# Stick-breaking scores: the second pass on half the rows, two key stretches in two halves of the array

## The chip, the cores and the metric

The kernel runs on one core of a Trainium2 chip, as one program. A core has five engines with instruction queues of their own: TensorE (PE in the profile; its weight loads are listed apart as PEld), VectorE (DVE), ScalarE (ACT), GpSimd (POOL) and SyncE (SP, which here only issues DMAs). They run side by side and wait for each other through semaphores. The metric is the device time of one execution in microseconds (us), the median of several runs. Before the change it is 1746.15 us (three runs, 1745.22 to 1746.89).

## The reference

The kernel is one decoder block on 1024 tokens of width 1024 in float32: three attention branches, gated and merged, and a squared-ReLU MLP. The change touches the first branch, stick-breaking attention, with 8 heads of 64 columns:

```python
def stick_breaking_attention(q, k, v):
    for i in range(s_len // BLOCK_Q):          # 8 tiles of 128 queries
        q0 = i * BLOCK_Q
        kend = q0 + BLOCK_Q
        z = einsum('bhtd,bhsd->bhts', q[:, :, q0:kend], k[:, :, :kend]) * HD ** -0.5
        strict = s_idx < t_idx
        log_rem = where(strict, log_sigmoid(-z), 0.0)
        after = cumsum(log_rem, reverse=True) - log_rem
        w = where(strict, exp(log_sigmoid(z) + after), 0.0)
        outs.append(einsum('bhts,bhsd->bhtd', w, v[:, :, :kend]))
```

Query tile i needs the scores of the keys 0 to 128(i+1), so tiles 0 to 3 need at most 512 keys and tiles 4 to 7 need 640 to 1024. The other branches are forgetting attention (8 heads, a softmax with a decay) and attention to 256 memory tokens.

## The kernel before

**Numbers in two parts.** Matmuls take the type float32r, which keeps fewer bits than float32. So every operand is split into a high part (rounded by ScalarE) and a rest (original less high part, made by VectorE), and a product is made of several passes: high by high, high by rest, rest by high. The dense layers use three passes with 128 contraction rows each (`passes`, line 1040 as `products`).

**Scores.** A head has only 64 columns, so the two parts of a query fit into one operand of 128 rows: `q` holds the high part in rows 0 to 63 and the rest in rows 64 to 127 (`put_queries`, lines 1169 and 1170). A key tile `k1` holds the key's high part twice, in both row halves (lines 1182 and 1183). So one matmul of `q` with `k1` (line 772) makes high by high plus rest by high. A second tile `k2` holds the key's rest, again in both halves (lines 1186 and 1187), and the second matmul of the group (line 773) adds `q` with `k2` to the same PSUM bank: high by rest, and rest by rest.

**Tiles and stretches.** `chunks(i)` cuts the keys of a query tile into stretches of at most 512, and a stretch of 128 is computed 256 wide. Tiles 0 to 3 have one stretch (256, 256, 384 and 512 wide), tiles 4 to 7 have two: 512, and then 256, 256, 384 and 512. `sb_tile` starts one process for each stretch (`chunk`): it takes one of the two SC banks, issues the two matmuls, VectorE adds the causal mask on the diagonal (line 782), ScalarE writes two sigmoids (lines 776 and 777), and the bank is free again. When both stretches are done, VectorE runs the product scan (line 791) and a multiplication (line 795). A unit (`unit`) is two query tiles of one head: after them come transposes on TensorE (line 874), splits of the transposed weights (lines 879 and 881), products with the values (line 894), the sum of the two halves of the result (lines 912 and 913) and a store. Eight pairs of heads, four stick-breaking and four forgetting, have 16 such tiles each. `fox_tile` is the forgetting branch's form; its second score matmul (line 816) uses 68 rows.

**Where operands live.** `HT` is a pool of 20 tiles of 128 x 512 for queries and keys. A stick-breaking pair takes 8 for keys (`k1`, `k2`, two heads, two halves of the sequence) and 4 for queries. `Pair.read` counts the units that still need a tile and gives it back. `sb_projection` may start when enough are free (`may`).

**The order of the work.** Up to the last branch the order is written out while the program is built, by a small planner. Processes are generators that yield `Op(engine, cost, fn)`, `Get(place, n)` (n tiles or banks of a pool) or `Sleep`. A `Machine` keeps a clock of its own, gives each engine the oldest ready Op, and calls `fn`, which issues the instructions; `mm_time`, `act_time` and `dve_time` are the planner's costs for widths. The result is a fixed instruction order for each engine. Dense projections and branch products are `side` work; `units` starts the next attention unit once the planner's count of side work has passed `PACE`, which places the pairs along the dense work. Units of large tiles (4 to 7) and of small ones come from two such processes. Score groups are one Op on PE each, so nothing comes between the matmuls of one `scores` call.

**DMAs.** All loads of weights and stores of head results are issued by SyncE; GpSimd issues only stores of the MLP stage. The change adds and removes none.

Of the kernel before, what the change touches and what calls it, by code (L numbers as in the profile page):

```python
# [17 lines left out]
AF = mybir.ActivationFunctionType  # L18
ALU = mybir.AluOpType
AX = mybir.AxisListType  # L20

P = 128
# [5 lines left out]
HD = 64  # L28
# [10 lines left out]
def f32(ap):  # L39
    return ap.bitcast(F32)  # L40
# [3 lines left out]
def tile_hybrid_block(  # L44
# [20 lines left out]
    nc = tc.nc  # L65
# [24 lines left out]
    def bank(tag):  # L90
        return psum.tile([P, 512], F32, tag=tag, name=nm(tag), bufs=PSB[tag])
# [81 lines left out]
    class Places:  # L173
# [4 lines left out]
        def put(self, *tiles):  # L178
            self.free.extend(tiles)
            machine.serve(self)  # L180

    class Machine:
# [12 lines left out]
        def spawn(self, gen, late=0.0):  # L195

            done = Event()
            proc = [gen, late, done, None]
            self.at(self.now, lambda: self.resume(proc, None))
            return done  # L200
# [82 lines left out]
    spawn = machine.spawn  # L283

    def mm_time(*cols):
        return sum(0.004 + 0.000445 * m for m in cols)

    def act_time(*cols):
        return sum(0.08 + 0.00083 * m for m in cols)

    def dve_time(*cols):
        return sum(0.08 + 0.00105 * m for m in cols)
# [27 lines left out]
    def chunks(i):  # L320

        res, n = [], P * (i + 1)
        for c in range(0, n, 512):
            m = min(512, n - c)
            res.append((c, max(m, 256), m))
        return res
# [8 lines left out]
    def banks(tag):  # L335
        return Places([bank(tag) for _ in range(PSB[tag])])
# [4 lines left out]
    PP, SC, TR, PV = (banks(tag) for tag in ("pp", "sc", "tr", "pv"))  # L341
    ES, OO = tiles(A, "es", 2, 512), tiles(A, "o", 3, 512)
    EL, RR, HT = Places([]), Places([]), Places([])
# [6 lines left out]
    def passes(a, b):  # L350
        return ((a[0], b[0]), (a[0], b[1]), (a[1], b[0]))
# [410 lines left out]

    def sb_tile(pair, b, i, beta):
        n = P * (i + 1)
        q = pair.t["q", b, i // 4][:, (i % 4) * P:(i % 4 + 1) * P]
        rho = yield Get(RR)

        def chunk(ci, c, m, u):
            sc = yield Get(SC)

            def scores():
                nc.tensor.matmul(sc[:, :m], q, pair.t["k1", b, ci][:, :m], start=True, stop=False)  # L772
                nc.tensor.matmul(sc[:, :m], q, pair.t["k2", b, ci][:, :m], start=False, stop=True)  # L773

            def sigmoids():
                nc.scalar.activation(rho[:, c:c + u], sc[:, :u], AF.Sigmoid, scale=-HD ** -0.5)  # L776
                nc.scalar.activation(beta[:, c:c + u], sc[:, :u], AF.Sigmoid, scale=HD ** -0.5)

            yield Op("PE", mm_time(m, m), scores)
            if c + u == n:  # L780
                dg = sc[:, u - P:u]
                yield Op("DVE", 0.22, lambda: nc.vector.tensor_tensor(dg, dg, strict, ALU.add))
            yield Op("ACT", act_time(u, u), sigmoids, table=AF.Sigmoid)
            SC.put(sc)

        for ev in [spawn(chunk(ci, *c), 0.5) for ci, c in enumerate(chunks(i))]:
            yield ev

        def scan():
            rev = rho[:, n - 1::-1] if n == D else rho[:, 0:n][:, ::-1]  # L790
            nc.vector.tensor_tensor_scan(out=rev, data0=rev, data1=zero.to_broadcast([P, n]),  # L791
                                         initial=1.0, op0=ALU.mult, op1=ALU.add)

        def weights():
            nc.vector.tensor_tensor(beta[:, 0:n - 1], beta[:, 0:n - 1], rho[:, 1:n], ALU.mult)

        yield Op("DVE", 0.1 + 0.00215 * n, scan, 0.14)
        yield Op("DVE", dve_time(n), weights)
        RR.put(rho)
# [124 lines left out]
    def units(large):  # L924
# [5 lines left out]
        for c, pair in enumerate(pairs):  # L930
            for n, (b, g) in enumerate(UNITS):
                if (g >= 2) != large:
                    continue
                es = yield Get(EL if large else ES, 2)
                while machine.side - base < PACE[c] + (PACE[c + 1] - PACE[c]) * n / 8:
                    yield Sleep(0.5)
# [99 lines left out]
    def products(ps, pairs_, first, last):  # L1036
        def fn():
            n = len(pairs_)
            for i, (a_, b_) in enumerate(pairs_):
                nc.tensor.matmul(ps, a_, b_, start=(first and i == 0), stop=(last and i == n - 1))  # L1040
        return fn
# [17 lines left out]
    def evict(last, gen, ps, place=PP):  # L1059
        def go():  # L1060
            yield last
            yield from gen
            place.put(ps)
        return spawn(go(), 1.0)
# [76 lines left out]
    def first_keys(weights, give, v_given):  # L1141

        w, = yield from weights(1)
        tiles_ = []
        put = put_keys(pairs[0], tiles_)

        def kept(ps, half):
            tiles_.extend((yield Get(HT, 4)))
            yield from put(ps, half)

        for t in range(4):
            if t % 2 == 0:
                ps = yield Get(SC)
            for s in (2 * t, 2 * t + 1):
                yield h_made[s]
            cs, out_ = slice(t * 256, t * 256 + 256), ps[:, (t % 2) * 256:(t % 2) * 256 + 256]
            for k in range(0, KD, 2):
                ab = [x_ for kk in (k, k + 1) for x_ in passes(tuple(a_[:, kk, :] for a_ in w), (hTh[:, kk, cs], hTl[:, kk, cs]))]
                last = yield Op("PE", 6 * mm_time(256), products(out_, ab, k == 0, k == KD - 2), side=True, goes_on=True)
            if t % 2:  # L1160
                evict(last, kept(ps, t // 2), ps, SC)
        give(last, slice(0, 1) if v_given.fired else slice(2, 3))

    def put_queries(pair, tiles_):
        def put(ps, half):
            for b in range(2):
                q = pair.t["q", b, half] = tiles_.pop()
                src = ps[b * HD:(b + 1) * HD, :]
                yield Op("ACT", act_time(512), lambda: nc.scalar.activation(q[:HD], src, AF.Copy))
                yield Op("DVE", dve_time(512), lambda: nc.vector.tensor_tensor(q[HD:], src, f32(q[:HD]), ALU.subtract))  # L1170
            machine.fire(pair.made["q", half])
        return put

    def put_keys(pair, tiles_):
        def put(ps, half):
            for b in range(2):
                k1, k2 = tiles_.pop(), tiles_.pop()
                pair.t["k1", b, half], pair.t["k2", b, half] = k1, k2
                src = ps[b * HD:(b + 1) * HD, :]

                def high():
                    nc.scalar.activation(k1[:HD], src, AF.Copy)
                    nc.scalar.activation(k1[HD:], src, AF.Copy)

                def low():
                    nc.vector.tensor_tensor(k2[:HD], src, f32(k1[:HD]), ALU.subtract)
                    nc.vector.tensor_tensor(k2[HD:], src, f32(k1[:HD]), ALU.subtract)
                yield Op("ACT", act_time(512, 512), high)
                yield Op("DVE", dve_time(512, 512), low)
            machine.fire(pair.made["k", half])  # L1190
        return put

    def sb_projection(c, keys):
        pair, tiles_ = pairs[c], []

        def may():
            n = 8 if keys else 4
            if len(HT.free) < n or c and not all(ev.fired for ev in mq_made.values()) or not keys and sb_taken[0] < 2 * c + 1 \
                    or keys and sb_taken[0] < 2 * c:
                return False  # L1200
            sb_taken[0] += 1
            tiles_.extend(HT.free.popleft() for _ in range(n))
            return True
        return dense_T((C_SBK if keys else C_SBQ) + c * P, (put_keys if keys else put_queries)(pair, tiles_), may)
# [327 lines left out]
        acc.extend(t[:, i, :] for t in acc2 for i in range(2))  # L1532
        machine.fire(closed)

    PACE = [62 * min(c, 4) + 58 * max(c - 4, 0) + 14 * (c == 8) for c in range(9)]
    with tc.manual_schedule():
        spawn(prologue())
        spawn(memory())
# [196 lines left out]
    with tc.manual_schedule():  # L1735
# [64 lines left out]
        spawn = machine.spawn  # L1800
        pps, scs = [bank("pp") for _ in range(3)], [bank("sc") for _ in range(2)]
# [13 lines left out]
        rows = [], []  # L1815
# [470 lines left out]
        q = {}  # L2286
# [48 lines left out]
        for k, (j, kind) in enumerate(plan):  # L2335
            n_ = groups[j][1]
            for t in range(4):
                ps = (bx if kind in ("P1", "P6", "P5", "P3") else by)[t]
                (sh, sl), (th, tl) = sop[k], top[k][:2]
                qs = slice(t * P, (t + 1) * P)  # L2340
                for c in range(n_):
                    for i, (a_, b_) in enumerate(((sh, th), (sh, tl), (sl, th))):
                        nc.tensor.matmul(ps, a_[:, c, qs], b_[:, c, :],  # L2343
                                         start=(kind in ("P1", "P2", "P7") and c == 0 and i == 0),
                                         stop=(kind in ("P2", "P4", "P3") and c == n_ - 1 and i == 2),
# [58 lines left out]
```

## Time and profile before

| | |
|---|---|
| median of three runs | 1746.15 us (1745.22 to 1746.89) |
| profiled execution, its own time | 1743.94 us |
| its span, first to last instruction | 1742.2 us |
| matmuls on TensorE | 9426, busy 1726.7 us |
| VectorE, ScalarE busy | 1262.0 us, 884.8 us |
| first and last score product of the stick-breaking heads (start) | 232.4 us, 586.3 us |
| score products of these heads | 96 first passes, 96 second passes |
| granted TensorE clock | 1.000 |

The profile is of one execution. Its page gives busy time by engine, and the trace can be asked for groups of instructions by line (count, busy time in us, mean ns of one, idle time ahead), for busy times in stretches of the span, for who waited for whom, and for a timeline with start and length of each instruction. L772 is line 772 of the kernel before; `sc<-h,h` means that a tile called sc is written from two tiles called h. The form `128*128 128x512` is a matmul with 128 contraction rows and 128 stationary columns, and a moving operand of 512 columns. The recorded end of a matmul is modelled and lies past the start of the next one, because matmuls are pipelined; how long one really occupies the array is the distance between starts.

### The profile page before, as it was taken

To read this page: it belongs to the slowest core of one execution; us is meant where nothing else is said; L and a number is where in the kernel's file an instruction comes from. 1 tells how busy PE (TensorE), PEld (TensorE's weight loads), DVE (VectorE), ACT (ScalarE), POOL (GpSimd) and SP (SyncE) were. 2 spreads that over 40 slices of the span, in tenths; PEclk is the share of its full clock that TensorE was granted. 3 is DMA by queue.
4 is the path that set the end of the run, shared out by engine and by line. 5 is a ranking of instruction groups with operands and counts; after the bars stand their busy time and mean duration, and the time that the engine had idled before them with its cause. 6 is when DMAs were issued, how large, how long until landed. Compare 5 with 4: busy or idle time off the path is not lost.

```text
span 1742.2 us, 24834 instructions
## 1 busy us (share of the span) xinstructions
PE 1726.7 (99%) x9426; PEld 1475.3 (85%) x9426; DVE 1262.0 (72%) x2014; ACT 884.8 (51%) x1553; POOL 115.1 (7%) x298
## 2 busy tenths in 40 slices
PE   9999999999999999999999999999999999999999
PEld 9889989888988899899888887878888877888887
DVE  7524578677777567666887699887777776687875
ACT  6525575555566478767974336533332344333331
POOL 0101100000000000010000000121112110000000
PEclk9999999999999999999999999999999999999999
DMA  5241121122132311212354643144344475455531
GB/s 206 73 125 51 50 87 38 42 68 58 36 87 58 90 54 32 78 54 60 117 173 138 225 163 116 43 159 155 133 152 151 145 271 212 156 201 180 194 121 73
DMA packets 136328, 201.41 MB, mean 116 GB/s; under 512 B 9680, under 2 KB 73168, under 8 KB 136208
## 3 DMA queue, kind: packets, MB, share of 16 engines
q1 hardware_dynamic: 127168, 170.20, 30.3%
q0 software_dynamic: 9040, 29.63, 4.9%
q8 instruction: 74, 1.21, 0.3%
q14 instruction: 46, 0.38, 0.1%
HBM read 142.64 MB, written 57.15 MB: 115 GB/s over the span
## 4 chain that ended last, share of the span: by engine, by line
PE 84%; issue 6%; DVE 4%; ACT 2%; POOL 2%; DMA 1%; SPq 0%; POOLq 0%; DVEq 0%; ACTq 0%
PE pp L1040 37%; PE pp L2343 7%; PE pp L1673 6%; PE pv L894 4%; PE tr L2343 4%; PE sc L2343 4%; PE tr L874 4%; PE sc L1673 3%; PE pv L2343 2%; POOL s_scr L1690 1%; PE tr L1673 1%; PE sc L772 1%; PE sc L773 1%; PE tr L1916 1%; PE sc L815 1%
## 5 line engine op out<-in xcount | busy, mean ns | idle before, releaser
L1040 PE MATMUL pp<-hi,whi 128*128 128x512 f32 x496 | 199.1, 401 | 0.0
L1040 PE MATMUL pp<-hi,wlo 128*128 128x512 f32 x496 | 195.8, 395 | 0.0
L1040 PE MATMUL pp<-lo,whi 128*128 128x512 f32 x496 | 195.1, 393 | 0.0
L1040 PE MATMUL pp<-whi,hi 128*128 128x256 f32 (+1 forms) x640 | 183.3, 286 | 0.0
L1040 PE MATMUL pp<-whi,lo 128*128 128x256 f32 (+1 forms) x640 | 179.8, 281 | 0.2 <-DVE lo L487 0.2
L1040 PE MATMUL pp<-wlo,hi 128*128 128x256 f32 (+1 forms) x640 | 179.2, 280 | 0.0
L2343 PE MATMUL pp<-h,sop 128*128 128x512 f32 x540 | 129.0, 395 | 2.3 <-DVE sop L1609 2.3
L881 DVE TENSOR_TENSOR ptl<-tr,pth 128x512 fp32r<-128x512 f32 (+1 forms) x160 | 99.3, 632 | 43.2 <-ACT pth L879 42.3
L2343 PEld LDWEIGHTS pp<-h,sop 128*128 128x128 f32 x540 | 101.1, 187 | 27.7 <-DVE sop L1609 2.6
L879 ACT ACTIVATE pth<-tr 128x512 fp32r<-128x512 f32 (+1 forms) x160 | 86.3, 555 | 70.1 <-PE tr L874 41.8
L1673 PE MATMUL pp<-h,oh 128*128 128x512 f32 x384 | 120.9, 396 | 0.7 <-ACT cu L1759 0.6
L1040 PEld LDWEIGHTS pp<-wlo,hi 128*128 128x128 f32 x640 | 120.5, 188 | 0.9
L1040 PEld LDWEIGHTS pp<-whi,hi 128*128 128x128 f32 x640 | 120.6, 188 | 0.8
L1040 PEld LDWEIGHTS pp<-whi,lo 128*128 128x128 f32 x640 | 120.4, 188 | 0.4 <-DVE lo L487 0.4
L1040 PEld LDWEIGHTS pp<-hi,wlo 128*128 128x128 f32 x496 | 93.1, 188 | 22.9 <-DVE wlo L951 0.3
L951 DVE TENSOR_TENSOR wlo<-raw,whi 128x1024 fp32r<-128x1024 f32 (+1 forms) x72 | 87.7, 1221 | 33.5 <-ACT whi L950 33.1
L1040 PEld LDWEIGHTS pp<-lo,whi 128*128 128x128 f32 x496 | 93.3, 188 | 16.8
L1040 PEld LDWEIGHTS pp<-hi,whi 128*128 128x128 f32 x496 | 93.3, 188 | 16.3
L791 DVE TENSOR_TENSOR_SCAN r<-r,sm 128x896 f32<-128x896 f32 (+3 forms) x64 | 86.2, 1351 | 13.0 <-ACT r L776 12.4
L950 ACT ACTIVATE whi<-raw 128x1024 fp32r<-128x1024 f32 (+1 forms) x72 | 76.2, 1061 | 33.4 <-DMA raw<-w_b 24.7
L1673 PEld LDWEIGHTS pp<-h,oh 128*128 128x128 f32 x384 | 71.7, 187 | 19.2 <-ACT cu L1759 1.5
L2261 ACT ACTIVATE h<-t 128x2048 fp32r<-128x2048 f32 x16 | 30.7, 1921 | 112.3 <-DVE t L1609 99.6
(423 smaller groups left out, 4278.8 us busy)
## 6 DMA issues: line engine op xcount, KB each, us to landing
ur<-s_scr SPq DMA_DIRECT2D x27, 1024.0 KB
raw<-w_in SPq DMA_DIRECT2D x42, 512.0 KB
raw<-w_up SPq DMA_DIRECT2D x60, 256.0 KB
s_scr<-s POOLq DMA_DIRECT2D x60, 256.0 KB, 2.7
g<-w_down SPq DMA_DIRECT2D x15, 1024.0 KB
gate_scr<-o SPq DMA_DIRECT2D x48, 256.0 KB
s_scr<-cu POOLq DMA_DIRECT2D x48, 256.0 KB, 2.9
o<-gate_scr SPq DMA_DIRECT2D x32, 256.0 KB
```

Of the source, the lines that this page charges most:

```text
L772: nc.tensor.matmul(sc[:, :m], q, pair.t["k1", b, ci][:, :m], start=True, stop=False)
L791: nc.vector.tensor_tensor_scan(out=rev, data0=rev, data1=zero.to_broadcast([P, n]), initial=1.0, op0=ALU.mult, op1=ALU.add)
L874: nc.tensor.transpose(tr[:, jj * 256 + a * P:jj * 256 + (a + 1) * P], es[a][:, j * P:(j + 1) * P], ident)
L879: yield Op("ACT", act_time(512 - lo_c), lambda: nc.scalar.activation(ph[:, lo_c:], tr[:, lo_c:], AF.Copy))
L881: yield Op("DVE", dve_time(512 - lo_c), lambda: nc.vector.tensor_tensor(pl[:, lo_c:], tr[:, lo_c:], f32(ph[:, lo_c:]), ALU.subtract))
L894: nc.tensor.matmul(pv[0][:, c_:256], v_of[key][:, j, h4, :], p_[:, jj * 256 + c_:(jj + 1) * 256], start=(k == 0 and n_ == 0 and i == 0), s ...
L950: yield Op("ACT", 0.03 + act_time(m), lambda: nc.scalar.activation(hi, raw, AF.Copy))
L951: yield Op("DVE", dve_time(m), lambda: nc.vector.tensor_tensor(lo, raw, f32(hi), ALU.subtract))
L1040: nc.tensor.matmul(ps, a_, b_, start=(first and i == 0), stop=(last and i == n - 1))
L1673: nc.tensor.matmul(ps, w[a_][:, k * P:(k + 1) * P], h[b_][k], start=(first and k == 0 and i == 0), stop=(last and k == 3 and i == 2), skip ...
L2261: nc.scalar.activation(top[k][0], raw, AF.Copy)
L2343: nc.tensor.matmul(ps, a_[:, c, qs], b_[:, c, :], start=(kind in ("P1", "P2", "P7") and c == 0 and i == 0), stop=(kind in ("P2", "P4", "P3 ...
```

## The change

The second pass of a stretch is cut to the 64 rows that multiply the query's high part by the key's rest; the product rest by rest is left out. Since the key's rest then fills only 64 rows, one tile `k2` holds both halves of the sequence: the rest of keys 0 to 511 in rows 0 to 63, that of keys 512 to 1023 in rows 64 to 127. For the second stretch the query's high part is needed in rows 64 to 127 as well, so the queries of tiles 4 to 7 get a second tile `q2` with a copy there. `scores` now issues both stretches of a tile as one Op, both first passes and then both second passes: the second pass of stretch 0 lies in rows 0 to 63 of the array, that of stretch 1 in rows 64 to 127. The tile takes both SC banks for it. Tiles 0 to 3 use the rows 0 to 63 alone. A pair needs 6 HT tiles for keys and 6 for queries. The planner's cost of a score group of two stretches is that of both first passes and one second pass of 512; PACE has new values.

```diff
@@ sb_tile
-        q = pair.t["q", b, i // 4][:, (i % 4) * P:(i % 4 + 1) * P]
+        ch = chunks(i)
+        qs = slice((i % 4) * P, (i % 4 + 1) * P)
+        q, k2 = pair.t["q", b, i // 4][:, qs], pair.t["k2", b, 0]
         rho = yield Get(RR)
+        scs = yield Get(SC, len(ch))
+        scs = scs if len(ch) == 2 else [scs]
+
+        def scores():
+            for ci, (c, m, u) in enumerate(ch):
+                nc.tensor.matmul(scs[ci][:, :m], q, pair.t["k1", b, ci][:, :m], start=True, stop=False)
+            for ci, (c, m, u) in enumerate(ch):
+                rows = slice(ci * HD, (ci + 1) * HD)
+                qh = pair.t["q2", b, 1][:, qs] if ci else q
+                nc.tensor.matmul(scs[ci][:, :m], qh[rows], k2[rows, :m], start=False, stop=True)
 
         def chunk(ci, c, m, u):
-            sc = yield Get(SC)
-
-            def scores():
-                nc.tensor.matmul(sc[:, :m], q, pair.t["k1", b, ci][:, :m], start=True, stop=False)
-                nc.tensor.matmul(sc[:, :m], q, pair.t["k2", b, ci][:, :m], start=False, stop=True)
+            sc = scs[ci]
...
-            yield Op("PE", mm_time(m, m), scores)
...
-        for ev in [spawn(chunk(ci, *c), 0.5) for ci, c in enumerate(chunks(i))]:
+        yield Op("PE", mm_time(512, *(m for _, m, _ in ch)) if len(ch) == 2 else mm_time(ch[0][1], ch[0][1]), scores)
+        for ev in [spawn(chunk(ci, *c), 0.5 * ci) for ci, c in enumerate(ch)]:
             yield ev
@@ first_keys
-            tiles_.extend((yield Get(HT, 4)))
+            tiles_.extend((yield Get(HT, 2 if half else 4)))
@@ put_queries
+                q2 = pair.t["q2", b, half] = tiles_.pop() if half else None
                 src = ps[b * HD:(b + 1) * HD, :]
-                yield Op("ACT", act_time(512), lambda: nc.scalar.activation(q[:HD], src, AF.Copy))
+
+                def high():
+                    nc.scalar.activation(q[:HD], src, AF.Copy)
+                    if half:
+                        nc.scalar.activation(q2[HD:], src, AF.Copy)
+                yield Op("ACT", act_time(512, 512) if half else act_time(512), high)
@@ put_keys
-                k1, k2 = tiles_.pop(), tiles_.pop()
-                pair.t["k1", b, half], pair.t["k2", b, half] = k1, k2
+                k1 = pair.t["k1", b, half] = tiles_.pop()
+                if half == 0:
+                    pair.t["k2", b, 0] = tiles_.pop()
+                k2 = pair.t["k2", b, 0]
...
-                    nc.vector.tensor_tensor(k2[:HD], src, f32(k1[:HD]), ALU.subtract)
-                    nc.vector.tensor_tensor(k2[HD:], src, f32(k1[:HD]), ALU.subtract)
+                    nc.vector.tensor_tensor(k2[half * HD:(half + 1) * HD], src, f32(k1[:HD]), ALU.subtract)
...
-                yield Op("DVE", dve_time(512, 512), low)
+                yield Op("DVE", dve_time(512), low)
@@ sb_projection
-            n = 8 if keys else 4
+            n = 6
@@
-    PACE = [62 * min(c, 4) + 58 * max(c - 4, 0) + 14 * (c == 8) for c in range(9)]
+    PACE = [52 * c for c in range(9)]
```

## The prediction

> **What bounds the kernel now.** I read the page's busy times first, then busy times by stage, then TensorE's own waits, and last its timeline around the score products.
>
> ```profile
> span 1742.2 us, 24834 instructions
> PE 1726.7 (99%) x9426; PEld 1475.3 (85%) x9426; DVE 1262.0 (72%) x2014; ACT 884.8 (51%) x1553; POOL 115.1 (7%) x298
> ```
>
> ```profile
> core 0: us, PE busy (x) PEld busy (x) DVE busy (x) ACT busy (x) POOL busy (x), PEclk, DMA share, GB/s
> 232.00:590.00 358.00, 358.00 (x2124) 313.83 (x2123) 273.93 (x405) 212.19 (x422) 4.11 (x13) 1.00 0.22 62
> 590.00:942.00 352.00, 348.98 (x2315) 316.50 (x2314) 249.96 (x601) 258.09 (x523) 19.11 (x84) 1.00 0.28 82
> ```
>
> The stage from 232 to 590 us holds all the stick-breaking heads, woven into dense projections. TensorE is busy in all of it (358.00 of 358); VectorE has 84 us to spare and ScalarE 146. The forgetting stage behind it has 3.0 us idle. TensorE's own waits, longest first (us in total, times, longest), agree:
>
> ```profile
> PE pp L2343 <- DVE sop L1609: 2.3, 1, 2.3
> PE tr L874 <- DVE ptl L881: 1.6, 1, 1.6
> PE tr L874 <- ACT es L846: 1.2, 1, 1.2
> ```
>
> No wait of a score product is in that list. So the time is the sum of what the matmuls occupy TensorE for. The recorded length of one (about 0.39 us at 512 columns) isn't that, since they overlap; the distance between starts is. The timeline has start, length, instruction:
>
> ```profile
> 302.57 0.42 PE L772 MATMUL sc<-h,h 128*128 128x384 f32 x1
> 302.83 0.34 PE L773 MATMUL sc<-h,h 128*128 128x384 f32 x1
> 303.00 0.39 PE L772 MATMUL sc<-h,h 128*128 128x512 f32 x1
> 303.23 0.39 PE L773 MATMUL sc<-h,h 128*128 128x512 f32 x1
> 303.46 0.28 PE L1040 MATMUL pp<-whi,hi 128*128 128x256 f32 x1
> 303.58 0.28 PE L1040 MATMUL pp<-wlo,hi 128*128 128x256 f32 x1
> ```
>
> A product of 512 columns holds TensorE 0.23 us (303.00 to 303.23), one of 384 0.17 (302.83 to 303.00), one of 256 0.12. The first of a group that follows transposes pays 0.26 in place of 0.17.
>
> **The change, part by part.** The two programs issue the same 9426 matmuls, of the same widths. What can differ is whether two second-pass products run at once, what the 64-row form costs, and where TensorE waits.
>
> *Pairs in the two halves.* The second passes that change are these (mean ns, then idle):
>
> ```profile
> L773 PE MATMUL sc<-h,h 128*128 128x512 f32 x48 | 18.9, 394 | 0.0
> L773 PE MATMUL sc<-h,h 128*128 128x256 f32 x32 | 8.9, 280 | 0.0
> L773 PE MATMUL sc<-h,h 128*128 128x384 f32 x16 | 5.4, 338 | 0.0
> L816 PE MATMUL sc<-h,h 68*128 68x512 f32 x48 | 19.1, 397 | 0.0
> ```
>
> Each of 8 heads has tiles 4 to 7 with a first stretch of 512 and a second of 256, 256, 384 and 512. If the second runs wholly beside the first, a head saves 0.12 + 0.12 + 0.17 + 0.23 = 0.64 us, all heads 5.1. The lower end is 0: no two products of this trace run at once. The weight load may cost part of it; loads in a stretch of narrow products, and those products, stand so:
>
> ```profile
> 304.60 0.19 PEld L894 LDWEIGHTS pv<-ptl,v 128*128 128x128 f32 x1
> 304.72 0.19 PEld L894 LDWEIGHTS pv<-pth,v 128*128 128x128 f32 x1
> 304.84 0.19 PEld L894 LDWEIGHTS pv<-ptl,v 128*128 128x128 f32 x1
> 304.95 0.19 PEld L1040 LDWEIGHTS pp<-whi,hi 128*128 128x128 f32 x1
> 305.06 0.19 PEld L1040 LDWEIGHTS pp<-wlo,hi 128*128 128x128 f32 x1
> ```
>
> ```profile
> 304.72 0.28 PE L894 MATMUL pv<-ptl,v 128*128 128x256 f32 x1
> 304.84 0.22 PE L894 MATMUL pv<-pth,v 128*128 128x128 f32 x1
> ```
>
> Loads come every 0.11 us at best, and the next load starts as a matmul starts (304.72, 304.84). If the upper half's load likewise waits until the lower half's product starts, the pair lasts 0.11 plus the second width: 0.23 at 256 (nothing lost), 0.28 at 384 (0.05 lost), 0.34 at 512 (0.11 lost). That is 0.16 a head, 1.3 in all, and 3.8 us saved. I take 3.8, since the rows show one load ahead and never two; 5.1 stays as an end.
>
> That two row tiles overlap at all, no row here shows. The Trainium skill ("TensorE: Matmul & The Clock Gate", Part 3) reports four products of 32 rows in one array running 3.07 times as fast as one by one; by that the saving is real, and without it this term is 0 and the sum that of the second rival. The forecast keeps the term because the halves share neither rows, operand partitions nor result bank.
>
> *Tiles 0 to 3.* Their 32 second passes use 64 rows alone, with nothing beside them. L816 with 68 rows takes 397 ns against 394 for L773 with 128, so fewer rows alone save nothing: 0.
>
> *Switching the form of the array.* Each of the 64 score groups now goes from 128 rows to 64 and back: 128 switches. The trace has one change of form, in columns: transposes with 8 active columns amid dense products.
>
> ```profile
> 474.74 0.39 PE L1040 MATMUL pp<-lo,whi 128*128 128x512 f32 x1
> 474.97 0.40 PE L1040 MATMUL pp<-hi,wlo 128*128 128x512 f32 x1
> 475.20 0.60 PE L1220 MATMUL tr<-ident,fn 128*8 128x128 f32 x4
> 475.56 0.48 PE L1040 MATMUL pp<-hi,whi 128*128 128x512 f32 x1
> 475.87 0.40 PE L1040 MATMUL pp<-lo,whi 128*128 128x512 f32 x1
> ```
>
> ```profile
> 309.54 0.93 PE L874 MATMUL tr<-ident,es 128*128 128x128 f32 x7
> 310.22 0.48 PE L1040 MATMUL pp<-hi,whi 128*128 128x512 f32 x1
> 310.53 0.39 PE L1040 MATMUL pp<-lo,whi 128*128 128x512 f32 x1
> ```
>
> The narrow form starts 0.23 after the last dense product, as any product would, and the way back (475.56, length 0.48, next start 0.31 on) is that of full-width transposes (310.22, 0.48, 0.31). So a switch costs nothing to see here, and I take 0. The upper end is a drained array: the recorded end of a product lies 0.39 − 0.23 = 0.16 us behind the moment the next would start, and a load that can't be made ahead adds 0.11; 128 × 0.27 = 34.6 us.
>
> The Trainium skill ("TensorEngine Tiling (Array Packing)", Key Properties) says that changing the tiling mode drains TensorE. The column rows above don't show that drain; rows of the array may differ, so the rule is the first rival.
>
> *Fewer, longer groups.* The scores stand in 68 unbroken groups on TensorE before and in 58 after, because both stretches of a tile go together. Ten breaks fewer save at most 10 × 0.09 (0.26 − 0.17), and perhaps a third of groups follow transposes: 0.3 us.
>
> *Copies.* Keys lose one of two subtractions in each of 16 places, queries gain 8 copies:
>
> ```profile
> L1187 DVE TENSOR_TENSOR h<-pp,h 64x512 fp32r<-64x512 f32 x12 | 8.3, 689 | 0.2
> L1183 ACT ACTIVATE h<-pp 64x512 fp32r<-64x512 f32 x12 | 7.1, 593 | 0.1
> ```
>
> VectorE gets 16 × 0.69 = 11.0 us less, ScalarE 8 × 0.59 = 4.7 more. What hides both is the dense work on TensorE; without that cover the 8 copies, in 4 puts, would lengthen the wait for a pair's late queries by 1.2 us each. Taken at 0.
>
> *Two score banks at once, pace, tiles.* A large tile now waits until both SC banks are free, and its first sigmoid starts behind four products in place of two (0.24 to 0.46 us later). Behind that ScalarE instruction queue copies and splits of other work; who waits is the transposes, L874. ScalarE's present wait there:
>
> ```profile
> ACT r L776 <- DVE sc L782: 19.0, 28, 2.0
> ```
>
> PACE ends at 416 in place of 494, yet in the new order scores run from matmul 1553 to 3779 (1564 to 3667 before), so it isn't the pace that holds them but banks and tiles. The last product of attention is number 6028 of TensorE in place of 5989, with 117 dense matmuls behind it until the branches' end in place of 156, at 0.23 us still 27 us of cover for the last store, load and split. No DMA is added (492 on SP in both). The edits with HT (6 and 6 tiles in place of 8 and 4) move projections, not their number. Bounds: the 3.0 us idle of 590 to 942 could all go; as much could come, in waits of 1.2 to 1.6 like the two shown. Taken at 0.
>
> Sum: 3.8 + 0.3 = 4.1 us off. The profiled execution took 1743.94 (span 1742.2 and 1.7 around it), which gives 1739.8; it was 2.2 under the median, so 1746.15 − 4.1 = 1742.0, 0.24% faster. I count 0.2% (3.5 us) as the least that a measurement of this kernel can tell from no change; three runs spread over 1.7.
>
> **Rivals.** *The array drains at each switch* (slower). Place: before the first 64-row product and after the last, in 64 groups. At 0.16 us that is 20.5, less 4.1: 16.4 more, 1762.5. With unprefetched loads 34.6 less 4.1: 1776.7. It decides from 4.1 / 128 = 32 ns a switch. Against it: the rows of L1220. For it: those are columns, and transposes. The Trainium skill's rule on modes, named above, would make this of the time.
>
> *The halves run one after the other.* Then 0.3 is left, 1745.9. For it: the trace has no two products at once, and 68 rows run no faster than 128. Against: nothing the two share.
>
> *Attention falls behind.* The pairing of banks costs waits before L874: three or four of 1.2 to 1.6 are about 5 us, less 4.1: 1747. For it: one bank pair serves all large tiles, and ScalarE already waits on the mask (L782). Against: 0.0 idle in the stage now.
>
> **How the numbers follow.** Forecast 0.50 (0.43 faster by over 0.2%, 0.07 within); drain 0.28 (0.27 slower, 0.01 within, where it is about 32 ns), of it 0.08 with loads; one after the other 0.12 (0.10 within, 0.02 slower); falling behind 0.10 (0.05, 0.05). Faster 0.43, same 0.23, slower 0.34. The range runs from full overlap with half the idle time gone (1746.15 − 5.1 − 1.5 = 1739.5) to the drained array (1763), leaving out the drain with loads and the edges. The forecast's own range is 1739.5 to 1744.
>
> **What would show it.** In the timeline a pair's second product starts about 0.11 after its first, not 0.23, and the next 128-row product 0.23 to 0.34 after the first. A start of the first 64-row product later than 0.23 behind a 512-wide one, or a long gap behind the pair, is the drain. New TensorE waits at the transposes are the third rival. I am wrong if a switch costs over 32 ns, or if pairs step by the full width.

## The result and the profile after

The changed kernel takes 1767.55 us (median of four runs, 1766.4 to 1767.7) against 1745.68 us for the kernel before beside it: 1.0125 times the time, interval 1.0107 to 1.0142. It is slower by 21.9 us; 1742.0 was forecast. The profiled execution has a span of 1765.9 us. The head of its page:

```profile
span 1765.9 us, 24847 instructions
PE 1748.8 (99%) x9426; PEld 1470.5 (83%) x9426; DVE 1253.2 (71%) x1998; ACT 890.1 (50%) x1561; POOL 118.5 (7%) x298
```

TensorE still fills the span, with the same 9426 matmuls. So they hold it longer, or it waits in a way that counts as busy. The waits that the profile names don't explain 21.9 us; the longest are these (us in total, times, longest; the lines behind the score products have moved by up to 15):

```profile
PE pp L1048 <- DVE wlo L959: 2.3, 4, 0.9
PE pp L2358 <- DVE sop L1624: 2.3, 1, 2.3
PE sc L823 <- ACT e L841: 1.2, 1, 1.2
```

The second passes are now L778. Their instructions, TensorE's idle time before them, and when the first and the last start:

```profile
L778 PEld LDWEIGHTS sc<-h,h x96: 182/183/183, 231.6 to 620.3; 64*128 64x128 f32 x96
L778 PE MATMUL sc<-h,h x96: 379/467/502, 231.6 to 620.3; 64*128 64x512 f32 x48, 64*128 64x256 f32 x32, 64*128 64x384 f32 x16
  issue: 15.3, 55
```

A row of 15.3 us put down to "issue", 55 times, is new: time in which the engine, here its weight loads, waited for nothing that the profile shows. L773 had no such row. One large tile's group on the timeline, products and then weight loads:

```profile
298.00 0.28 PE L902 MATMUL pv<-ptl,v 128*128 128x256 f32 x1
298.12 0.51 PE L774 MATMUL sc<-h,h 128*128 128x512 f32 x2
298.56 0.49 PE L778 MATMUL sc<-h,h 64*128 64x512 f32 x2
298.99 0.51 PE L1048 MATMUL pp<-hi,whi 128*128 128x512 f32 x1
299.33 0.39 PE L1048 MATMUL pp<-lo,whi 128*128 128x512 f32 x1
299.56 0.39 PE L1048 MATMUL pp<-hi,wlo 128*128 128x512 f32 x1
```

```profile
298.56 0.19 PEld L778 LDWEIGHTS sc<-h,h 64*128 64x128 f32 x2 [0.25 <-issue]
298.99 0.19 PEld L1048 LDWEIGHTS pp<-hi,whi 128*128 128x128 f32 x1 [0.24 <-issue]
299.09 0.19 PEld L1048 LDWEIGHTS pp<-lo,whi 128*128 128x128 f32 x1
299.33 0.19 PEld L1048 LDWEIGHTS pp<-hi,wlo 128*128 128x128 f32 x1
```

The two first passes, 512 and 256 wide, begin at 298.12 and should be through at 298.47 (0.23 + 0.12). The 64-row products start at 298.56, 0.09 late, and their loads only then: within a stream of one form a load starts together with the product before it, here it waits. Both 64-row loads and both products then go as one (x2). The next load of 128 rows starts at 298.99, 0.43 later, again not ahead of time, and the load behind that one 0.11 later, when its product really starts; the product after it follows at 299.33, 0.34 on in place of 0.23. So I read the 0.43 as a load of 0.11, a stream of 0.23 (the products themselves) and a gap of 0.09. A round trip into the 64-row form costs about twice 0.09 and twice 0.11, 0.40 us, while this pair saves the 0.12 of its second width.

### The profile page after: what moved, and what is told of

It reads as the page before. It is cut to its first block, busy times and chain, and to the rows that moved or that the text cites. A ratio compares the mean times of both kernels' runs of the same rounds, so it can differ in the third digit from the quotient of the medians.

```text
span 1765.9 us, 24847 instructions
## 1 busy us (share of the span) xinstructions
PE 1748.8 (99%) x9426; PEld 1470.5 (83%) x9426; DVE 1253.2 (71%) x1998; ACT 890.1 (50%) x1561; POOL 118.5 (7%) x298
## 4 chain that ended last, share of the span: by engine, by line
PE 82%; issue 7%; DVE 5%; ACT 2%; POOL 2%; DMA 1%; SPq 0%; POOLq 0%; DVEq 0%; ACTq 0%
PE pp L1048 37%; PE pp L2358 7%; PE pp L1688 6%; PE pv L902 4%; PE tr L882 4%; PE tr L2358 3%; PE sc L2358 3%; PE sc L1688 3%; PE pv L2358 2%; POOL s_scr L1705 1%; PE sc L778 1%; PE tr L1688 1%; PE sc L774 1%; DVE h L1624 1%; PE sc L823 1%
## 5 line engine op out<-in xcount | busy, mean ns | idle before, releaser
L1048 PE MATMUL pp<-hi,whi 128*128 128x512 f32 x496 | 202.8, 409 | 0.0
L799 DVE TENSOR_TENSOR_SCAN r<-r,sm 128x128 f32<-128x128 f32 (+3 forms) x64 | 86.2, 1351 | 10.4 <-ACT r L784 10.1
L958 ACT ACTIVATE whi<-raw 128x1024 fp32r<-128x1024 f32 (+1 forms) x72 | 76.3, 1061 | 25.8 <-DMA raw<-w_b 11.5
```

The source lines that it names most:

```text
L958: yield Op("ACT", 0.03 + act_time(m), lambda: nc.scalar.activation(hi, raw, AF.Copy))
```

## The experiments

Theory A: each change between the 128-row and the 64-row form drains the array, that is, the next form waits until the products of the last one are out (0.09 us), and it keeps the next weight load from being made ahead (0.11 us). Theory B: what the change does to score banks, order and pace makes TensorE wait. All times stand against the kernel before, run on the same chip (1744.7 to 1745.2 us).

### Second passes of 128 rows in the changed kernel

```diff
-                nc.tensor.matmul(scs[ci][:, :m], qh[rows], k2[rows, :m], start=False, stop=True)
+                nc.tensor.matmul(scs[ci][:, :m], qh, k2[:, :m], start=False, stop=True)
...
+                    if half:
+                        nc.vector.tensor_tensor(q2[:HD], src, f32(q[:HD]), ALU.subtract)
```

> The changed kernel in its own order, banks, pace and tiles, but every second pass is again a product of 128 rows: stretch 0 multiplies the whole query tile by the shared key-rest tile, stretch 1 multiplies q2, whose rows 0 to 63 now hold the query's rest. What the added rows contribute is rest by rest, below the rounding of the result. It goes without the 64-row form and without any overlap of the two halves. Theory A (each change between 128 and 64 rows costs TensorE about 0.09 us of drain and 0.11 us of a weight load that can't be made ahead, 0.40 us for each of 64 groups): the 19 us that are lost by the last score product go, 1744 to 1750 us. Theory B (the pair of banks, the new order and pace make TensorE wait): as slow as the changed kernel, 1764 to 1768 us.

Measured: 1748.52 us against 1744.89, ratio 1.0021 (1.0012 to 1.0030). Of the 21.9 us, 18.3 are gone with the 64-row form, as theory A has it; 3.6 stay, and they belong to something else. In the waits of this run those for the rest of dense weights (`wlo`) are longer in total, and one for `g` has come; the kernel before has one wait for `wlo`, shown behind them. Over the whole span TensorE idles 17.4 us here (1748.0 less 1730.6 busy) and 15.5 before, so waits make about 1.9 of the 3.6; where the rest goes isn't shown.

```profile
PE pp L1048 <- DVE wlo L959: 2.8, 6, 0.9
PE sc L823 <- ACT e L841: 1.1, 1, 1.1
PE pp L1048 <- DVE g L1504: 0.9, 1, 0.9
```

```profile
PE pp L1040 <- DVE wlo L951: 1.2, 1, 1.2
```

### 64 rows for the pairs alone

```diff
                 rows = slice(ci * HD, (ci + 1) * HD)
+                rows = rows if len(ch) == 2 else slice(0, P)
```

> The changed kernel with 64 rows for the pairs of tiles 4 to 7 alone: the second pass of tiles 0 to 3 is a product of 128 rows again (rest by rest in the added rows). Theory A: 32 of 64 round trips go, 32 x 0.40 = 12.8 us less than the changed kernel, near 1755 us; the 5.1 us of overlap stay in. Theory B: no different from the changed kernel, 1767 us.

Measured: 1755.86 us, ratio 1.0063 (1.0050 to 1.0077). That is 11.0 over before and 10.9 under the changed kernel, for 32 round trips fewer (0.34 each, where 0.40 was expected). Against the full-row run it is 7.3 slower. Its pairs save 5.0 by overlap (below), so its 32 trips cost 12.3, or 0.39 us each. Even where every trip carries a pair, the form loses.

### 64 rows in the kernel before, nothing paired

```diff
-                nc.tensor.matmul(sc[:, :m], q, pair.t["k2", b, ci][:, :m], start=False, stop=True)
+                nc.tensor.matmul(sc[:, :m], q[:HD], pair.t["k2", b, ci][:HD, :m], start=False, stop=True)
```

> The kernel before with one edit: each of its 96 second passes uses rows 0 to 63 alone (rest by rest is left out). Nothing is paired, and order, banks and pace are those of before. Theory A: 96 round trips x 0.40 = 38 us more than before, near 1784 us. Theory B, and any theory in which the pairing is what costs: as before, 1746 us.

Measured: 1783.27 us, ratio 1.0220 (1.0202 to 1.0239): 38.4 us for 96 trips, 0.40 each. Banks, order and pace are untouched here, so theory B can't make it. A group of two stretches on its timeline:

```profile
302.41 0.44 PE L772 MATMUL sc<-h,h 128*128 128x512 f32 x1
302.78 0.50 PE L773 MATMUL sc<-h,h 64*128 64x512 f32 x1
303.21 0.38 PE L772 MATMUL sc<-h,h 128*128 128x256 f32 x1
303.53 0.38 PE L773 MATMUL sc<-h,h 64*128 64x256 f32 x1
```

The step from a 64-row product of 512 columns to the next product is 0.43 (302.78 to 303.21), and from there the 256-wide first pass takes 0.32 in place of 0.12.

### The overlap taken away

Both second passes of a tile use rows 0 to 63 here, one behind the other; the rest of the upper keys is left out.

```diff
-                rows = slice(ci * HD, (ci + 1) * HD)
-                qh = pair.t["q2", b, 1][:, qs] if ci else q
+                rows = slice(0, HD)
+                qh = q
```

> The changed kernel with the overlap taken away: the second stretch's second pass uses rows 0 to 63 too (of the first stretch's key rest, so the rest of the upper keys is replaced by a wrong one, a change in the last digits of the scores). Same number of 64-row products, same switches. If the two halves of the array really ran at once and saved whole second widths, the 5.1 us come back: 1772 to 1773 us. If the overlap was worth nothing, 1767 to 1768; if the upper half's load had held it back, about 1771.5.

Measured: 1772.01 us, ratio 1.0156 (1.0141 to 1.0172): 26.9 over before, where the changed kernel is 21.9 over it. The overlap is worth 5.0 us. One group of two 512-wide stretches, in the changed kernel and then in this one:

```profile
242.76 0.50 PE L778 MATMUL sc<-h,h 64*128 64x512 f32 x2
243.19 0.50 PE L1048 MATMUL pp<-hi,whi 128*128 128x512 f32 x1
```

```profile
243.11 0.73 PE L778 MATMUL sc<-h,h 64*128 64x512 f32 x2
243.77 0.50 PE L1048 MATMUL pp<-hi,whi 128*128 128x512 f32 x1
```

In two halves the pair holds TensorE 0.43 us, in one half 0.66: the difference is the whole second width, 0.23.

### Is it the rows, and what of it is the load?

Three kernels add one short product (128 moving columns) between first and second pass to each of the 96 groups of the kernel before: with 128 rows and 32 stationary columns, with 64 rows and 128 columns, and with 64 rows and 32 columns.

```diff
+                nc.tensor.matmul(sc[:32, :P], q[:, :32], pair.t["k2", b, ci][:, :P], start=False, stop=False, skip_group_check=True)
```

```diff
+                nc.tensor.matmul(sc[:, :P], q[:HD], pair.t["k2", b, ci][:HD, :P], start=False, stop=False)
```

```diff
+                nc.tensor.matmul(sc[:32, :P], q[:HD, :32], pair.t["k2", b, ci][:HD, :P], start=False, stop=False, skip_group_check=True)
```

> The kernel before with an extra product in each of 96 score groups, between first and second pass: 128 rows, 32 stationary columns, 128 moving columns (it adds the key's rest once more for 32 queries and 128 keys, so the output is changed in its last digits). It asks whether the column form costs what the row form does. If only row forms drain the array (as the 8-column transposes of the profile before let one think): 96 x 0.06 to 0.11 = 6 to 11 us more than before, 1752 to 1757 us. If every change of form does: another 96 x 0.40 = 38 us, near 1792 us.

> The kernel before with an extra product in each of 96 score groups, between first and second pass: 64 rows, 128 stationary and 128 moving columns (the key's rest counted twice for 128 keys, a change in the last digits). It is the row form's counterpart to the extra product of 128 rows and 32 columns, which cost 0.10 us each. If a round trip into the row form costs twice 0.09 of drain and twice 0.11 of load, with 0.06 for the product: 96 x 0.46 = 44 us more than before, 1789 us. If it is the shortness of a product with fewer active cells and not the rows: 10 us, 1755 us.

> As the kernel with the extra product of 64 rows, but with 32 stationary columns in place of 128, so that the load on the way in is short. If the load on the way in stands exposed as part of the price (0.11 us for 128 columns), 0.07 to 0.08 us a trip goes: 7 us less, near 1782 us. If the price is the drain alone and loads stay hidden: the same as with 128 columns.

Measured: 1754.71 us (ratio 1.0057, 1.0038 to 1.0075), 1787.17 (1.0241, 1.0221 to 1.0261) and 1779.55 (1.0198, 1.0178 to 1.0218). The column form costs 9.8 / 96 = 0.10 us a product, the row form 42.5 / 96 = 0.44. The timelines of these two kernels, the column form first, around a 256-wide stretch:

```profile
281.72 0.28 PE L772 MATMUL sc<-h,h 128*128 128x256 f32 x1
281.84 0.23 PE L773 MATMUL sc<-h,h 128*32 128x128 f32 x1
281.90 0.33 PE L774 MATMUL sc<-h,h 128*128 128x256 f32 x1
282.07 0.28 PE L1041 MATMUL pp<-whi,hi 128*128 128x256 f32 x1
```

```profile
287.37 0.28 PE L772 MATMUL sc<-h,h 128*128 128x256 f32 x1
287.58 0.32 PE L773 MATMUL sc<-h,h 64*128 64x128 f32 x1
287.83 0.39 PE L774 MATMUL sc<-h,h 128*128 128x256 f32 x1
288.06 0.28 PE L1041 MATMUL pp<-whi,hi 128*128 128x256 f32 x1
```

Into the column form the step is 0.12, that of any 256-wide product; into the row form 0.21. With 32 columns in place of 128 the row form gets 7.6 us cheaper, 0.08 a trip, close to the 7 expected for a load that nothing hides. The loads of the extra product in the two kernels (128 columns, then 32; ns least, median, most) are 0.08 us apart as well, while the idle time ahead of them is the same (23.8 us in 85 places), so it is the load that got cheaper and not the drain:

```profile
L773 PEld LDWEIGHTS sc<-h,h x96: 182/183/183, 232.9 to 629.2; 64*128 64x128 f32 x96
  issue: 23.8, 85
L773 PEld LDWEIGHTS sc<-h,h x96: 102/103/103, 232.7 to 621.4; 64*32 64x32 f32 x96
  issue: 23.8, 85
```

So the row form is the cause, and a load on the way in is part of the price. The load on the way out wasn't varied; its share rests on the loads of the timeline.

Not every product on fewer than 128 rows pays the price. The forgetting branch's second pass has 68 rows and pays nothing in the kernel before, on the way in or out (0.24 and 0.23 from start to start):

```profile
649.80 0.40 PE L815 MATMUL sc<-h,h 128*128 128x512 f32 x1
650.04 0.40 PE L816 MATMUL sc<-h,h 68*128 68x512 f32 x1
650.27 0.39 PE L1040 MATMUL pp<-hi,whi 128*128 128x512 f32 x1
```

The program asks for an array tile of 64 x 128 for the 64-row products, of 128 x 32 for those of 32 columns, and of the full 128 x 128 for those of 68 rows, as for the dense ones.

### Pace and banks

The 3.6 us of the full-row run have two candidates. One kernel is the one before with the new PACE, the other the full-row kernel with the old PACE:

```diff
-    PACE = [62 * min(c, 4) + 58 * max(c - 4, 0) + 14 * (c == 8) for c in range(9)]
+    PACE = [52 * c for c in range(9)]
```

> The kernel before with the changed kernel's PACE alone. The full-row run left 3.6 us (0.2%) that neither switches nor overlap explain. If the pace is their cause (attention packed more densely, weights of dense tasks late): about 1748 to 1749 us. If the pairing of the two score banks is: as before, 1745 us.

> The full-row kernel (changed kernel, second passes of 128 rows, rest by rest in the added rows) with the PACE of before. If the pace cost the 3.6 us: 1745 us. If the pairing of banks, with both stretches in one group, does: 1748 to 1749 us.

Measured: 1745.86 us (ratio 1.0004, 0.9995 to 1.0013) and 1756.62 (1.0066, 1.0053 to 1.0079). Both guesses on the second missed: with the old pace the paired banks and tiles cost not 3.6 but 11.5 us. The pace alone does nothing to the kernel before, but takes 8 of the 11.5 back in the paired one. The forgetting stage of the full-row kernel with the old pace and with the new one (stretch, then busy times; the third number from the end is the granted clock), and the old-pace kernel's waits:

```profile
590.00:942.00 352.00, 344.31 (x2260) 311.26 (x2260) 242.97 (x577) 248.29 (x503) 18.71 (x84) 0.99 0.27 83
```

```profile
590.00:942.00 352.00, 349.01 (x2263) 313.23 (x2262) 250.59 (x598) 254.20 (x520) 19.22 (x72) 1.00 0.28 83
```

```profile
PE tr L882 <- ACT e L854: 3.0, 2, 2.0
PE pv L902 <- DVE ob L921: 2.2, 1, 2.2
PE tr L882 <- DVE ptl L889: 2.1, 1, 2.1
PE tr L882 <- ACT es L854: 1.2, 1, 1.2
```

TensorE idles 7.7 us there in place of 3.0, in waits for the transposes and products of late attention units; over the whole span it idles 20.7 in place of 17.4. Idle time is not all of the 8 us. At two of these waits, 2.10 and 1.98 us long, the old-pace profile has a stretch of 3.41 us in which the granted clock is halved:

```profile
870.39:873.80 3.41, 3.04 (x14) 3.04 (x15) 3.41 (x6) 3.26 (x6) 0.43 (x2) 0.50 0.52 175
928.42:931.83 3.41, 3.37 (x12) 2.98 (x13) 3.05 (x7) 3.10 (x9) 0.00 (x0) 0.50 0.31 103
```

The five runs of the old-pace kernel had a granted clock of 0.996 to 0.998 over their span, 0.997 in the median, those of the new pace 0.999 in the median. By that difference I estimate 0.002 x 1756 = 3.5 us for the lower clock, which with 3.3 of idle time makes 6.8 of the 8. Which of the pairing's parts does it, the two banks, the tile counts or the joint group, wasn't tried apart.

## Why the prediction was wrong

**The step that failed** is "switching the form of the array", taken at 0. It measured 0.40 us a round trip where nothing else differs (38.4 / 96), 0.39 with pairs, and (26.9 − 3.6) / 64 = 0.36 in the changed kernel without overlap. That is about 0.20 us a switch, where the prediction's own limit was 0.032. The sum as the runs give it: 3.6 for the rearrangement, 23.3 for 64 trips, 5.0 less for the overlap, 21.9 in all. The 23.3 is what the other two leave; 64 trips at 0.40 would be 25.6, and why a trip costs a little less here wasn't tried.

The zero came from L1220, the one change of form in the trace, and that was read rightly: the column form really carries no such price, as the extra product of 32 columns shows. What was wrong was to carry it over to rows. The prediction named that difference and still gave the row form the column form's price. The upper end, 0.27 a switch, was a drain of 0.16 and a load of 0.11. The load was right; the drain is 0.09, so the recorded end of a matmul was too late a mark for the moment from which the array takes another form. The range left out the drain with exposed loads (1776.7), and the result lies between the two drain prices, 1762.5 and 1776.7. The rival had the right place and mechanism.

The Trainium skill's rule that changing the mode drains the engine ("TensorEngine Tiling (Array Packing)", Key Properties) agrees with the row form here, at 0.09 us and a load that isn't made ahead; it doesn't agree with the column form of 32, which shows no drain.

**Pairs in the two halves**: the mechanism was right, the size too small. Taken was 3.8, with the upper half's load held back until the lower half's product starts. The pair starts as one (x2 within 298.56), and the overlap is worth 5.0, the end of 5.1. That products of different row groups run at once, as the Trainium skill says ("TensorE: Matmul & The Clock Gate", Part 3), holds for two halves of 64 rows.

**Tiles 0 to 3**: "0" for fewer rows was right of the product itself, but each carries a trip: taking the form from them alone won 10.9 us back.

**Two score banks, pace, tiles**: taken at 0 with bounds of 3.0 either way; the net is 3.6, so just outside. It hides a cost of 11.5 that the new pace mostly makes up for. That the pace doesn't hold the scores was wrong for the full-row kernel with its paired banks: its last score product starts at 587.9 us with the old pace and at 602.3 with the new one, and with the old pace it is 8 us slower. The third rival, waits at the transposes, shows there alone; in the changed kernel these waits are 0.5 us each, and the sign that the prediction named for it is missing.

**Copies** at 0, **fewer groups** at 0.3: not tried by themselves; both lie inside the 3.6.

## What to carry to other kernels

Work on half the rows of the array really doubles up, but here every stretch of it paid a drain and an exposed weight load on both sides, 0.40 us, against 0.12 to 0.23 us that a pair saves. By these numbers, as an estimate that no run tried, it would pay from two pairs of 512 or four of 256 on that follow each other in one form. A price seen for one kind of form (columns) is no evidence for the other (rows): put a short product of the very form in question into the stream before building on it. And when a planner's resources change, judge the change with its pace tuned and untuned, since the new pace hid 8 us of the pairing's cost here.

## What the runs showed of the hardware

A change between 128 and 64 contraction rows costs TensorE about 0.20 us each way (0.09 until the array is free, 0.11 for a weight load of 128 columns that doesn't overlap); with 32 stationary columns the trip is 0.08 us cheaper. Products of 68 rows pay nothing: 0.24 and 0.23 us from start to start around one of 512 columns. A change to 32 stationary columns and back costs no such thing: 0.10 us for the short product and all. Two 64-row products in the two halves start together and last as long as the longer one: 0.43 us for two of 512 columns with load and gap, 0.66 in one half. At TensorE waits of 2.10 and 1.98 us the old-pace profile shows the granted clock at 0.50 for 3.41 us each.
